# The residual of layer 1, turned in squares of 32 by VectorE at the end of layer 0, stored by token and loaded in rows

## The chip, the cores and the metric

The kernel runs on one core of one Trainium2 chip. The metric is the time of one execution on the device, in microseconds, as the median of several runs. Times that have a place in the program come from one profiled execution, and count from that execution's first instruction.

## The reference: two layers of a hybrid decoder trunk

1024 tokens with 1024 features pass through two layers. Layer 0 mixes the tokens by gated linear attention, layer 1 by a sparse attention in which an indexer picks 256 keys for each query. After each mixer the residual is added, normed, and given a gated term of its own:

```python
ALPHA = (2 * DEPTH) ** 0.25
...
for i in range(DEPTH):
    kind = i % N_MIXERS
    ...
    if kind == 0:
        y = gla_mixer(...)
    elif kind == 1:
        y = dsa_mixer(...)
    x = layer_norm(ALPHA * x + y, ln_g[i], ln_b[i])
    x = x + (p[i] @ ple_w[i]) * jax.nn.sigmoid(x @ ple_gate_w[i])
```

The change concerns the `x` that layer 0 leaves on this last line, and the term `ALPHA * x` of the line above it in layer 1. Both `dsa_mixer`'s output and the residual go into one sum per token, and `layer_norm` divides that sum by its own deviation, with a small constant under the root.

## The kernel before

**Tiling.** The tokens are worked on in two halves of 512 (`NH`, `HT`). The program is: layer 0 for the first half, layer 0 for the second, layer 1 for the first half, layer 1 for the second. An activation in "feature-major" form is eight tiles (`NK`) of 128 features x 512 tokens; these feed TensorE as operands. A matmul in near-f32 precision takes each operand as a high and a low part, which `split` makes: ScalarE copies a tile into the rounded type (the high part, L418), and VectorE subtracts that copy from the source (the low part, L410). A tile of `XT`, `x` in the profile's names, is such a pair. The sums that layer norm works on are "by token" instead: `y` is one tile of 128 tokens x 4 groups of tokens x 1024 features, so that a token's features lie in one partition. Going from the one form to the other needs a transposition.

**Layer 0's tail.** `tail` runs per half. It norms `y`, turns it back to feature-major tiles (`xpose`, TensorE, then L883 or L885), and then goes through eight gate blocks `b`, each 24 matmuls of 128x512 (`fm_block`). Behind a block, ScalarE applies the sigmoid, VectorE multiplies and adds (`gated`, L906 to L907), and `final` takes the finished feature-major tile `t` of layer 0's output. `final` (L1316) stores it into the DRAM tile `x2s` and splits it into the pair `X` that layer 1's first blocks read.

**Layer 1's residual.** Layer 1 runs in 16 slots per half, one for each head `h`, with matmul blocks of projections between the attention's own steps. In the slots 0 to 3 `residual` (L1442) loads two feature-major tiles back from `x2s` into `xst` tiles (256 KB each), lets TensorE transpose each in four 128x128 pieces into one PSUM bank (L1453, L62 in the profile), and lets ScalarE copy the bank into `y`, times `ALPHA` (L1454). After a slot's pair `st["y"]` counts up, and `dsa_out`, which adds the mixer's output into `y`, starts only when it has reached `NK` = 8. `norm_steps` then takes `y` with the constant `EPS`.

**What sets the order.** There is no scheduler: each engine runs its instructions in the order in which the Python program emits them. An object `fl` (`Flow`) keeps a modelled time `fl.now`, which every emitted matmul advances. Small steps are put on a heap with a due time (`fl.at`, `after`, and `chain`, a list of steps with the delay before the next), and are emitted between matmul blocks once their time has come. Two calls force what is on the heap out early: `fl.need(...)` emits steps until a condition holds, `fl.drain()` until the heap is empty. `fl.drain()` stands at the end of the second half's layer 0 (L1369); at the end of the first half there is none, and layer 1's small projections of that half (`small_head`) follow at once.

**What goes through SP.** All DMAs are issued by SyncE (SP) in program order. Of those that the prediction speaks of: `Weights` streams the weights' parts in (`whi` and `wlo` from `whs` and `wls`, L174); `split_ahead` (L213) prepares split weights in the background of layer 0, by a load of a raw piece `pst` (L223), ScalarE's copy `phi`, a store to `whs` (L235), VectorE's subtraction and a store to `wls` (L239), each store waiting for its engine; `small_head` loads the two rotary tables (L966 and L967, from `rope_s`; called `v` in the first half and `ix` in the second, by the tile that they take); L1644 loads the first half's keys `kI` in the second half.

**The rotary chain.** `small_head` projects the indexer's key and four blocks of its queries. `rope` turns each with the tables: two products and a shuffle on VectorE (L953 to L955), an addition (L958), then the split. Blocks of TensorE that use the results come some 40 us later.

Of the kernel before, what the change touches and what calls it, by code (L numbers as in the profile page):

```python
# [10 lines left out]
F32 = mybir.dt.float32  # L11
# [9 lines left out]
D = 1024  # L21
L = 1024
NH = 2
HT = 512
# [23 lines left out]
class Flow:  # L48
# [23 lines left out]
    def chain(self, *steps):  # L72

        (_, first), rest = steps[0], steps[1:]
        first()
        if rest:
            self.after(rest[0][0], lambda: self.chain((0, rest[0][1]), *rest[1:]))
# [200 lines left out]
def trunk_kernel(ctx, tc, x_tok, x_T, p_T, pos, freq, g_q, g_k, g_v, g_z, g_a, g_a2, g_ba, g_gn, g_o,  # L278
# [118 lines left out]

    x2s = dp.tile([NK, 128, L], F32, name="x2s")
    rope_s = dp.tile([4, 128, L], F32, name="rope_s")
    kv_s = dp.tile([6, 128, HT], F32, name="kv_s")  # L400
    sc_s = dp.tile([3, 128, L], F32, name="sc_s")

# [606 lines left out]
    def small_kv(half, X, f32t, alloc, tmp, spsum, kh, kl, vh, vl, res):  # L1009
        hs = slice(half * HT, half * HT + HT)  # L1010
        ch, sh = alloc(F32), alloc(F32)
        nc.sync.dma_start(ch[0:32], rope_s[0, 0:32, hs])
        nc.sync.dma_start(sh[0:32], rope_s[1, 0:32, hs])
        kf, vf = f32t(), f32t()

        def ev_k(ps):
            def done():
                res["k"] = True
            act.activation(kf, ps, AF.Copy)
            rope(kf[0:32], ch[0:32], sh[0:32], swap_h, tmp, lambda: split(kh, kl, kf, done))  # L1020

        yield from fm_block(("dk",), X, ev_k)

        def ev_v(ps):
            def turn():
                pt = spsum()
                for t in range(4):
                    fl.transpose(pt[:, t * 128:t * 128 + 128], vf[:, t * 128:t * 128 + 128], ident)

                def done():  # L1030
                    res["v"] = True
                split(vh, vl, pt, done)
            chain((0, lambda: act.activation(vf, ps, AF.Copy, scale=0.5)), (1.2, turn))

        yield from fm_block(("dv",), X, ev_v)

# [193 lines left out]
    for half in range(NH):  # L1230
# [82 lines left out]

        X = XT()

        def final(b, t, X=X, hs=hs):  # L1316
            nc.sync.dma_start(x2s[b, :, hs], t)
            X.put(b, t)
        turned = cycle((("U", 2), ("o", 1), ("U", 2), ("oT", 1), ("tr", 1)))

        def tps():
# [117 lines left out]
                X.put(*got)  # L1439
            yield  # L1440

    def residual(st, y, half, ks, start, end):  # L1442

        tiles = {}

        def load(k):
            tiles[k] = xp.tile([128, HT], F32, tag="xst", name="xst", bufs=2)
            nc.sync.dma_start(tiles[k], x2s[k, :, half * HT:(half + 1) * HT])

        def by_token(k):  # L1450
            ps = pbank()
            for t in range(4):
                fl.transpose(ps[:, t * 128:t * 128 + 128], tiles[k][:, t * 128:t * 128 + 128], ident)  # L1453
            act.activation(y[:, :, k * 128:k * 128 + 128], ps.rearrange("p (t c) -> p t c", c=128), AF.Copy,  # L1454
                           scale=ALPHA)
            st["y"] = k + 1

        for i, k in enumerate(ks):
            fl.at(start + 0.6 * i, lambda k=k: load(k))
            fl.at(end - 3.6 + 1.6 * i, lambda k=k: by_token(k))  # L1460

    def attend(st, h, half, ap, sq):

# [152 lines left out]
                                     [store(i) for i in range(nb)], [load(i) for i in range(nb)], [inverse, to_all])]  # L1616

    def dsa_out(st, js, ch, y, norm=None, ahead=1):
        fl.need(lambda: st.get("y") == NK)
        parts = [W.take(("do", j, ch)) for j in js]  # L1620

        def U(t, b):
# [78 lines left out]
    for half in range(NH):  # L1701
# [11 lines left out]
        for h, units in enumerate(plan, -1):  # L1713
# [36 lines left out]
            if h == 0:  # L1750
                y = xp.tile([128, 4, D], F32, tag="y", name="y")
            if 0 <= h < 4:
                residual(st, y, half, (2 * h, 2 * h + 1), start + 1.3, start + dur)
            fl.run(*(unit(u) for u in units))
        norm, y_done = norm_steps(y, l1, EPS, (0, 1))
        if half == 0:
            X = XT()
            feed_by(feed_x2(X, 1), fl.now + 21.0, 2.3)
# [80 lines left out]
```

## Time and profile before

| | before |
|---|---|
| time, median of 3 runs (lowest, highest) | 1962.26 us (1962.2, 1963.73) |
| the profiled execution, from its first to its last instruction | 1962.1 us |
| mean granted TensorE clock in it | 0.999 |
| HBM read, written | 331.18 MB, 131.99 MB |

The line of engines in the page (shown in the prediction) gives the busy time of each, with its share of the span. The page also cuts the span into 40 slices of 49 us; in each row a digit is the busy share in tenths, and the last two rows are the share of time in which the 16 DMA engines were busy and the rate at which they moved bytes:

```profile
PE   9999999999999999999999999999999999999999
DVE  5776676687778887877858987768797987777873
ACT  5664646446465646464545676766443553434432
DMA  4566565668757656656676588877866998888874
GB/s 153 185 184 212 190 215 181 215 183 263 249 186 236 210 194 195 211 180 209 209 260 250 181 309 289 275 264 267 317 216 234 362 317 295 297 302 276 291 272 145
```

Layer 0 ends for the first half at about 495 us (slice 11) and for the second at about 1025 us (slice 21); the residual's transposes in layer 1 lie between 1127 and 1593 us. TensorE is busy in every slice. In a row of a timeline, the columns are the start, the busy time, the engine, the line of the kernel, the operation, what it wrote and read, the tiles' shapes, and in brackets how long the engine had been idle before, and what ended that.

### The profile page before, as it was taken

How to read it: one execution, taken by the hardware profiler on the slowest of the kernel's cores; microseconds unless marked ns; L12 is line 12 of the kernel's file. 1: busy time of each engine (PE TensorE's matmuls, PEld its weight loads, DVE VectorE, ACT ScalarE, POOL GpSimd, SP SyncE). 2: the span in 40 equal slices, each digit the busy share in tenths (PEclk: the TensorE clock that was granted, in tenths of full speed). 3: DMA queues.
4: the chain of work that ended last, by engine and by line, in shares of the span. 5: the costliest groups of instructions: out<-in, count | busy, mean ns of one | idle time of the engine just before them, and what ended most of it. 6: DMA issues, size and time to landing. Idle time of an engine off the chain costs nothing.

```text
span 1962.1 us, 26826 instructions
## 1 busy us (share of the span) xinstructions
PE 1948.5 (99%) x9060; PEld 1614.2 (82%) x9060; DVE 1490.0 (76%) x3039; ACT 1021.7 (52%) x1928; POOL 53.6 (3%) x115
## 2 busy tenths in 40 slices
PE   9999999999999999999999999999999999999999
PEld 7888888888888888888888888888878888888877
DVE  5776676687778887877858987768797987777873
ACT  5664646446465646464545676766443553434432
POOL 0000000010000000000100000000000000000000
PEclk9999999999999999999999999999999999999999
DMA  4566565668757656656676588877866998888874
GB/s 153 185 184 212 190 215 181 215 183 263 249 186 236 210 194 195 211 180 209 209 260 250 181 309 289 275 264 267 317 216 234 362 317 295 297 302 276 291 272 145
DMA packets 174218, 464.96 MB, mean 237 GB/s; under 512 B 20096, under 2 KB 21120, under 8 KB 167936
## 3 DMA queue, kind: packets, MB, share of 16 engines
q1 hardware_dynamic: 174080, 463.25, 70.6%
q8 instruction: 71, 1.16, 0.2%
q14 instruction: 67, 0.55, 0.1%
HBM read 331.18 MB, written 131.99 MB: 236 GB/s over the span
## 4 chain that ended last, share of the span: by engine, by line
PE 93%; DVE 3%; ACT 2%; issue 1%; DMA 0%; SPq 0%; DVEq 0%; ACTq 0%
PE pb L58 70%; PE o L58 8%; PE U L58 6%; PE S L58 6%; PE oT L62 1%; PE tr L58 1%; DVE bn L828 0%; DVE y L786 0%; PE S L62 0%; ACT x L885 0%; DMA y<-in_x_T 0%; PE pb L62 0%; DVE sc L1067 0%; PE tr L62 0%; PE xt L62 0%
## 5 line engine op out<-in xcount | busy, mean ns | idle before, releaser
L58 PE MATMUL pb<-x,whi 128*128 128x512 f32 x2272 | 707.2, 392 | 0.0
L58 PEld LDWEIGHTS pb<-x,whi 128*128 128x128 f32 x2272 | 417.1, 188 | 79.5 <-DVE x L410 0.4
L58 PE MATMUL pb<-x,wlo 128*128 128x512 f32 x1136 | 443.1, 390 | 0.0
L58 PE MATMUL pb<-whi,u 128*128 128x512 f32 x1024 | 342.3, 394 | 0.1
L58 PEld LDWEIGHTS pb<-x,wlo 128*128 128x128 f32 x1136 | 213.3, 188 | 46.2 <-DVE wlo L191 0.4
L58 PEld LDWEIGHTS pb<-whi,u 128*128 128x128 f32 x1024 | 192.4, 188 | 40.8 <-ACT u L418 0.5
L58 PE MATMUL pb<-wlo,u 128*128 128x512 f32 x512 | 200.5, 392 | 0.0
L191 DVE TENSOR_TENSOR wlo<-wst,whi 128x512 fp32r<-128x512 f32 x232 | 154.5, 686 | 44.2 <-ACT whi L189 43.8
L189 ACT ACTIVATE whi<-wst 128x512 fp32r<-128x512 f32 x232 | 136.5, 622 | 81.7 <-DMA wst<-in_g_k 28.4
L1506 ACT ACTIVATE sq<-P,mx 128x128 f32<-128x128 f32 (+7 forms) x128 | 99.0, 774 | 89.3 <-DVE mx L1499 54.1
L1552 ACT ACTIVATE ph<-PT 128x512 fp32r<-128x512 f32 (+1 forms) x160 | 93.9, 601 | 63.5 <-PE o L58 44.6
L58 PE MATMUL S<-kT,q 128*128 128x512 f32 (+2 forms) x576 | 121.8, 343 | 0.0
L1550 DVE TENSOR_TENSOR PT<-PT,ph 128x512 fp32r<-128x512 f32 (+1 forms) x160 | 102.3, 649 | 17.7 <-ACT ph L1552 17.2
L58 PEld LDWEIGHTS S<-kT,q 128*128 128x128 f32 x576 | 100.5, 188 | 17.8 <-DVE mx L1499 0.7
L58 PEld LDWEIGHTS pb<-wlo,u 128*128 128x128 f32 x512 | 96.3, 188 | 18.8 <-DMA wlo<-wls 0.3
L1133 ACT ACTIVATE tk<-sc,tki 128x768 f16<-128x768 f32 (+2 forms) x90 | 92.8, 1031 | 22.9 <-DVE tki L1142 19.1
L58 PE MATMUL o<-ph,vT 128*128 128x512 f32 (+2 forms) x384 | 103.2, 353 | 0.2 <-ACT ph L1552 0.2
L1512 DVE STREAM_TRANSPOSE sq<-sq 128x128 f32<-128x128 f32 (+7 forms) x128 | 97.9, 769 | 4.0 <-ACT sq L1506 3.7
L731 ACT ACTIVATE junk<-o 128x512 bf16<-128x512 f32 x32 | 19.1, 597 | 152.1 <-DVE ot L729 141.0
L237 DVE TENSOR_TENSOR pst<-pst,phi 128x512 fp32r<-128x512 f32 x130 | 89.3, 687 | 5.4 <-ACT phi L233 5.0
L58 PE MATMUL pb<-whi,x 128*128 128x512 f32 x256 | 86.2, 395 | 0.4 <-DVE x L410 0.4
L58 PE MATMUL U<-whi,x 128*128 128x512 f32 x256 | 84.9, 391 | 0.0
(318 smaller groups left out, 3362.0 us busy)
## 6 DMA issues: line engine op xcount, KB each, us to landing
whi<-whs SPq DMA_DIRECT2D x128, 512.0 KB
wlo<-wls SPq DMA_DIRECT2D x128, 512.0 KB
sqd<-sq SPq DMA_DIRECT2D x192, 256.0 KB
PT<-sqd SPq DMA_DIRECT2D x48, 1024.0 KB
whs<-phi SPq DMA_DIRECT2D x130, 256.0 KB
wls<-pst SPq DMA_DIRECT2D x130, 256.0 KB
wst<-in_g_z SPq DMA_DIRECT2D x32, 512.0 KB
wst<-in_g_o SPq DMA_DIRECT2D x32, 512.0 KB
```

What stands on the lines that cost most here:

```text
L58: self.pe.matmul(out, lhsT, rhs, start=start, stop=stop)
L62: self.pe.transpose(out, in_, ident)
L189: self.nc.scalar.activation(hi[:, c], st[:, c], AF.Copy, scale=1.0 if gain is None else gain)
L191: self.nc.vector.tensor_sub(lo[:, c], st[:, c], hi[:, c].bitcast(F32))
L237: self.nc.vector.tensor_sub(st, st.bitcast(F32), hi.bitcast(F32))
L731: act.activation(junk, ps, AF.Square, accum_out=u["ss"][:, c:c + 1])
L1133: act.activation(junk()[:, :n], scs[j], AF.Sign, bias=cand[:, j:j + 1].bitcast(F32), accum_out=cnt[:, j:j + 1])
L1506: act.activation(to, rows, AF.Exp, scale=-1.0, bias=mx, accum_out=sm[:, t:t + 1])
L1512: dve.transpose(x, x)
L1550: dve.tensor_sub(lo, lo.bitcast(F32), hi.bitcast(F32))
L1552: chain((0, lambda: act.activation(hi, lo.bitcast(F32), AF.Copy)), (0.8, second))
```

## The change

In layer 0's tail, `final` now has a step more per tile. VectorE transposes the finished tile in squares of 32x32 into a tile `sq` (named `ah` in the profile, four buffers), and four DMAs store it to a new DRAM tile `yr_s`, by token. Squares alone do not transpose a tile: the rest is in the addresses of the stores, each of which takes 32 partitions (the tokens of one place in a square) with 16 pieces of 32 floats, and writes each piece into the row of its token. A store thus moves 64 KB in 512 pieces of 128 bytes. The turn has a due time 1.8 us of modelled time after `final`, the stores 2.2 us after the turn; both halves together have 16 turns and 64 such stores. The `x2s` store stays.

In layer 1, `residual` is now one load of 512 KB per slot 0 to 3, which brings 128 tokens' rows of 1024 features straight into `y`. The `xst` tiles, the 16 groups of four transposes and the 16 evictions are gone. `y` now holds `x` and not `ALPHA` times `x`; to make up for it, the values `V` are scaled by `0.5 / ALPHA` instead of 0.5, and the norm's constant is `EPS / ALPHA ** 2`. `dsa_out` starts when four loads are emitted.

```diff
--- before.py
+++ after.py
@@ -397,6 +397,7 @@
 
     x2s = dp.tile([NK, 128, L], F32, name="x2s")
     rope_s = dp.tile([4, 128, L], F32, name="rope_s")
+    yr_s = dp.tile([NH, 4, 4, 32, D], F32, name="yr_s")
     kv_s = dp.tile([6, 128, HT], F32, name="kv_s")
     sc_s = dp.tile([3, 128, L], F32, name="sc_s")
 
@@ -1030,7 +1031,7 @@
                 def done():
                     res["v"] = True
                 split(vh, vl, pt, done)
-            chain((0, lambda: act.activation(vf, ps, AF.Copy, scale=0.5)), (1.2, turn))
+            chain((0, lambda: act.activation(vf, ps, AF.Copy, scale=0.5 / ALPHA)), (1.2, turn))
 
         yield from fm_block(("dv",), X, ev_v)
 
@@ -1313,9 +1314,17 @@
 
         X = XT()
 
-        def final(b, t, X=X, hs=hs):
+        def final(b, t, X=X, hs=hs, half=half):
             nc.sync.dma_start(x2s[b, :, hs], t)
             X.put(b, t)
+            sq = t2k("ah", F32, 4)
+
+            def out():
+                for a in range(4):
+                    c = b * 128 + 32 * a
+                    nc.sync.dma_start(yr_s[half, :, :, :, c:c + 32].rearrange("t g c i -> c (t g) i"),
+                                      sq[32 * a:32 * a + 32].rearrange("p (n i) -> p n i", i=32))
+            chain((0, lambda: None), (1.8, lambda: dve.transpose(sq, t)), (2.2, out))
         turned = cycle((("U", 2), ("o", 1), ("U", 2), ("oT", 1), ("tr", 1)))
 
         def tps():
@@ -1439,25 +1448,12 @@
                 X.put(*got)
             yield
 
-    def residual(st, y, half, ks, start, end):
-
-        tiles = {}
-
-        def load(k):
-            tiles[k] = xp.tile([128, HT], F32, tag="xst", name="xst", bufs=2)
-            nc.sync.dma_start(tiles[k], x2s[k, :, half * HT:(half + 1) * HT])
-
-        def by_token(k):
-            ps = pbank()
-            for t in range(4):
-                fl.transpose(ps[:, t * 128:t * 128 + 128], tiles[k][:, t * 128:t * 128 + 128], ident)
-            act.activation(y[:, :, k * 128:k * 128 + 128], ps.rearrange("p (t c) -> p t c", c=128), AF.Copy,
-                           scale=ALPHA)
-            st["y"] = k + 1
-
-        for i, k in enumerate(ks):
-            fl.at(start + 0.6 * i, lambda k=k: load(k))
-            fl.at(end - 3.6 + 1.6 * i, lambda k=k: by_token(k))
+    def residual(st, y, half, t, start):
+
+        def load():
+            nc.sync.dma_start(y[:, t], yr_s[half, t].rearrange("g c d -> (g c) d"))
+            st["y"] = t + 1
+        fl.at(start, load)
 
     def attend(st, h, half, ap, sq):
 
@@ -1616,7 +1612,7 @@
                                      [store(i) for i in range(nb)], [load(i) for i in range(nb)], [inverse, to_all])]
 
     def dsa_out(st, js, ch, y, norm=None, ahead=1):
-        fl.need(lambda: st.get("y") == NK)
+        fl.need(lambda: st.get("y") == 4)
         parts = [W.take(("do", j, ch)) for j in js]
 
         def U(t, b):
@@ -1750,9 +1746,9 @@
             if h == 0:
                 y = xp.tile([128, 4, D], F32, tag="y", name="y")
             if 0 <= h < 4:
-                residual(st, y, half, (2 * h, 2 * h + 1), start + 1.3, start + dur)
+                residual(st, y, half, h, start + 1.3)
             fl.run(*(unit(u) for u in units))
-        norm, y_done = norm_steps(y, l1, EPS, (0, 1))
+        norm, y_done = norm_steps(y, l1, EPS / ALPHA ** 2, (0, 1))
         if half == 0:
             X = XT()
             feed_by(feed_x2(X, 1), fl.now + 21.0, 2.3)
```

**TensorE, slot 0 of layer 1 in the first half.** The rows are matmuls: `pb<-x,whi` and `pb<-x,wlo` are projections (PSUM bank from tile and weight), `pb<-ident,xst` the residual's transposes, `o<-...` the attention's output. Before:

```order
L58 MATMUL pb<-x,whi 128x512 x2
L58 MATMUL pb<-x,wlo 128x512
L62 MATMUL pb<-ident,xst 128x128 x4
L58 MATMUL o<-ph,vT_9810 128x512
L58 MATMUL o<-ph,vT_9811 128x512
L58 MATMUL o<-PT,vT_9810 128x512
L58 MATMUL pb<-x,whi 128x512 x2
L58 MATMUL pb<-x,wlo 128x512
L62 MATMUL pb<-ident,xst 128x128 x4
L58 MATMUL o<-ph,vT_9810 128x4x96
```

With the change:

```order
L58 MATMUL pb<-x,whi 128x512 x2
L58 MATMUL pb<-x,wlo 128x512
L58 MATMUL o<-ph,vT_9907 128x512
L58 MATMUL o<-ph,vT_9908 128x512
L58 MATMUL o<-PT,vT_9907 128x512
L58 MATMUL pb<-x,whi 128x512 x2
L58 MATMUL pb<-x,wlo 128x512
L58 MATMUL o<-ph,vT_9907 128x4x96
```

The two groups of transposes are gone, and the matmuls around them follow each other in the same order.

**SP, the end of the second half's layer 0.** The rows are DMAs in the order of issue: the weights of the last gate blocks, the stores of layer 0's last output tiles, then layer 1's first loads. Before:

```order
L174 DMA whi<-whs 128x1024
L174 DMA wlo<-wls 128x1024
L1317 DMA x2s<-x_9413 128x512
L1317 DMA x2s<-x_9423 128x512
L1644 DMA kI<-kv_s 128x512 x2
L966 DMA ix<-rope_s 128x512
L967 DMA ix<-rope_s 128x512
```

With the change:

```order
L174 DMA whi<-whs 128x1024
L174 DMA wlo<-wls 128x1024
L1325 DMA yr_s<-ah 32x16x32 x4
L1318 DMA x2s<-x_9462 128x512
L1318 DMA x2s<-x_9472 128x512
L1325 DMA yr_s<-ah 32x16x32 x8
L1640 DMA kI<-kv_s 128x512 x2
L967 DMA ix<-rope_s 128x512
```

The drain at L1369 brings out the stores of the last two tiles, eight in a row, between the last `x2s` store and the loads of `kI` and `ix`; the four of the tile before them stand ahead of the last two `x2s` stores.

**SP, the end of the first half's layer 0.** Here background stores and loads of `split_ahead` lie between the rest, and `v<-rope_s` is the rotary load. Before:

```order
L1317 DMA x2s<-x_4193 128x512
L235 DMA whs<-phi 128x512
L223 DMA pst<-in_d_z 128x512
L239 DMA wls<-pst 128x512
L174 DMA whi<-whs 128x1024
L174 DMA wlo<-wls 128x1024
L1317 DMA x2s<-x_4214 128x512
L235 DMA whs<-phi 128x512
L223 DMA pst<-in_d_z 128x512
L966 DMA v<-rope_s 128x512
```

With the change:

```order
L1325 DMA yr_s<-ah 32x16x32 x4
L1318 DMA x2s<-x_4194 128x512
L235 DMA whs<-phi 128x512
L223 DMA pst<-in_d_z 128x512
L239 DMA wls<-pst 128x512
L174 DMA whi<-whs 128x1024
L174 DMA wlo<-wls 128x1024
L1325 DMA yr_s<-ah 32x16x32 x4
L1318 DMA x2s<-x_4215 128x512
L235 DMA whs<-phi 128x512
L223 DMA pst<-in_d_z 128x512
L967 DMA v<-rope_s 128x512
```

A group of four turned stores now stands ahead of each `x2s` store from the second tile's on; six groups, 24 stores, come ahead of `v<-rope_s`, and the last two behind it.

## The prediction

> **What bounds the kernel now.** I read the page first, then the rows of the two edited places: TensorE's transposes in the first four slots of layer 1, and the end of layer 0 in each half with what follows it.
>
> ```profile
> span 1962.1 us, 26826 instructions
> PE 1948.5 (99%) x9060; PEld 1614.2 (82%) x9060; DVE 1490.0 (76%) x3039; ACT 1021.7 (52%) x1928; POOL 53.6 (3%) x115
> PE 93%; DVE 3%; ACT 2%; issue 1%; DMA 0%; SPq 0%; DVEq 0%; ACTq 0%
> ```
>
> TensorE is busy for 1948.5 of 1962.1 us and makes up 93% of the chain that ended last. So work taken from TensorE's stream comes off the time in full, and a delay elsewhere costs only what reaches TensorE. The sum is made against this execution's span of 1962.1 us; the median of the runs, 1962.26, lies 0.16 above it.
>
> **What is removed.** The first row counts the transposes of all residual tiles (minimum, median and largest duration in ns). The five after it are TensorE's timeline at the first and at the third residual group.
>
> ```profile
> L62 PE MATMUL pb<-ident,xst x64: 270/272/276, 1126.9 to 1593.3; 128*128 128x128 f32 x64
> ...
> 1126.68 0.39 PE L58 MATMUL pb<-x,wlo 128*128 128x512 f32 x1
> 1126.91 0.60 PE L62 MATMUL pb<-ident,xst 128*128 128x128 f32 x4
> 1127.26 0.72 PE L58 MATMUL o<-ph,vT 128*128 128x512 f32 x2
> ...
> 1143.00 0.60 PE L62 MATMUL pb<-ident,xst 128*128 128x128 f32 x4
> 1143.80 0.73 PE L58 MATMUL o<-ph,vT 128*128 128x512 f32 x2 [0.19 <-ACT ph L1552]
> ```
>
> The 272 ns of one transpose overlap with the next. What a group of four costs is the distance between the starts around it: 1127.26 - 1126.91 = 0.35 us. There are 64 / 4 = 16 groups, so TensorE's stream gets 16 x 0.35 = **5.6 us** shorter. At 1143.80 TensorE also sat idle for 0.19 us because ScalarE was late with `ph`; ScalarE's evictions of the residual, which go too, stand in front of it:
>
> ```profile
> L1454 ACT ACTIVATE y<-pb x16: 577/598/601, 1127.5 to 1593.6; 128x512 f32<-128x512 f32 x16
> L1512 DVE STREAM_TRANSPOSE sq<-sq 128x512 f32<-128x512 f32 x16 | 11.3, 707 | 3.6 <-ACT sq L1506 3.6
> ```
>
> I count 0.2 us for that. The rest of ScalarE's 16 x 0.598 = 9.6 us gives nothing, since ScalarE is busy for 52% of the span and TensorE does not wait for it there. Taken away in all: **5.8 us**.
>
> **What is added to VectorE.** 16 turns of 128x512. The second row has VectorE turning squares of that size in 707 ns, so 16 x 0.707 = 11.3 us. They fall into the last matmul blocks of layer 0:
>
> ```profile
> 455.00:460.00 5.00, 5.00 (x24) 4.14 (x23) 4.35 (x8) 3.67 (x6) 0.00 (x0) 1.00 0.71 247
> ...
> 493.00:498.00 5.00, 5.00 (x24) 4.14 (x23) 2.08 (x3) 0.97 (x2) 0.00 (x0) 1.00 1.02 356
> 500.00:510.00 10.00, 10.00 (x45) 8.26 (x44) 7.03 (x13) 3.58 (x6) 0.00 (x0) 1.00 1.03 404
> ```
>
> The third busy figure is VectorE's: 4.35 of 5 us at the start of the gate blocks, 2.08 at their end. One turn in each block of about 5.4 us fits into the idle rest, and each stands behind the low part that TensorE needs. VectorE's own time costs nothing. If it were full there, a turn would cost up to 0.7 us a block.
>
> **What is added to SP's queue, second half.** In the code each tile's four stores come late in the next block. At the end of the second half's layer 0 the program is drained: the turned stores of the last two tiles, eight in a row, come ahead of layer 1's first loads (the order's rows under the change). Before, SP and then VectorE and TensorE had there:
>
> ```profile
> 1017.54 5.76 SPq L1317 DMA_DIRECT2D x2s<-x  x2
> 1023.39 0.89 SPq L1644 DMA_DIRECT2D kI<-kv_s  x2
> 1024.33 0.42 SPq L966 DMA_DIRECT2D ix<-rope_s  x1
> ...
> 1023.65 0.69 DVE L410 TENSOR_TENSOR x<-x,x 128x512 fp32r<-128x512 f32 x1 [0.70 <-ACT x L418]
> 1029.41 0.68 DVE L953 TENSOR_TENSOR rt<-z,ix 64x512 f32<-64x512 f32 x1 [5.07 <-DMA ix<-rope_s]
> ...
> 1049.29 0.69 DVE L953 TENSOR_TENSOR rt<-z,ix 128x512 f32<-128x512 f32 x1 [0.19 <-ACT z L997]
> ...
> 1054.73 0.68 DVE L953 TENSOR_TENSOR rt<-z,qf 32x512 f32<-32x512 f32 x1 [0.55 <-ACT z L1019]
> ...
> 1070.49 0.69 DVE L410 TENSOR_TENSOR x<-y,x 128x512 fp32r<-128x512 f32 x1
> ...
> 1071.23 0.19 PEld L58 LDWEIGHTS pb<-x,whi 128*128 128x128 f32 x1 [0.36 <-DVE x L410]
> ...
> L1525 SPq DMA_DIRECT2D sqd<-sq x192: 303/601/1854, 1092.7 to 1869.3; - x192
> ```
>
> VectorE already waits 5.07 us for the rotary tables `ix`, whose load SP issues at 1024.33. With two `kI` issues in 0.89 us, one issue takes 0.45 us. The last tile's low part ends at 1023.65 + 0.69 = 1024.34 and its turn at 1025.05. The first four stores go from 1023.4 to 1025.2, the other four to 1027.0, so `kI` and then `ix` are issued 3.6 us later, and VectorE's wait ends 3.6 us later. What can take that up? Between 1029.41 and 1071 VectorE's only waits that are not part of the rotary chain itself are the 0.19 and the 0.55 us on ScalarE's evictions; of the 29 rows between 1054.73 and the low part at 1070.49 none has a wait. TensorE already waits 0.36 us for that low part. So 3.6 - 0.74 = **2.9 us** reach TensorE. From both sides: 0 if some of VectorE's queue can be caught up after all (the lag then ends in its idle time), and 4.1 with the 0.60 us median of the four-part stores `sqd<-sq` (8 x 0.6 = 4.8, less 0.74). I take 2.9 because the issue rows of that very place carry it.
>
> **Added to the DMA engines, first half.** Each store moves 64 KB as 32 x 16 pieces of 128 bytes, 32 pieces for each of 16 engines. No row shows a store in such pieces; the nearest is the small-piece loads at the kernel's start, in the stretch from 12.0 to 13.3 us:
>
> ```profile
> DMA packets 302, 0.10 MB, mean 77 GB/s; under 512 B 213, under 2 KB 280, under 8 KB 302
> ...
> q1 hardware_dynamic: 302, 0.10, 30.5%
> ...
> q1 hardware_dynamic: 174080, 463.25, 70.6%
> ...
> DMA packets 5290, 12.38 MB, mean 310 GB/s; under 512 B 590, under 2 KB 590, under 8 KB 5287
> ...
> SPq L223 <- DMA wls<-pst: 11.7, 6, 2.9
> ```
>
> 30.5% of 16 x 1.3 us over 302 packets is 21 ns each, with some 2-KB and larger ones in the mean: at most 32 x 0.021 = 0.67 us a store if a small store is like a small load. By bytes alone, at the 404 GB/s of the row of 500 to 510, it is 0.16 us. By the mean packet of the whole run (70.6% of 16 x 1962.1 us over 174080 = 127 ns) it is 4.1 us. I take **0.4 us**, the middle of the two nearest.
>
> The Trainium skill ("DMA: Bandwidth & Descriptors", "Specifications") says that transfers below 512 bytes miss the line rate because they are read, modified and written. If that doubled the 0.67 us, an estimate by this page, a store would take 1.3 us; no row of this trace shows a small store.
>
> 24 such stores stand ahead of the first half's rotary load (SP, 493 us): 24 x 0.4 = 9.6 us. The last but one row is the stretch from 460 to 500: 310 GB/s of the 404 seen, so 23% of the 33 us before 493, 7.7 us, are free, but SP spends 11.7 us of the same stretch (last row) waiting for a store of `wls` to land before it issues more, and a longer queue lengthens each of those waits. I count half of the free time and get a lag of 9.6 - 3.9, about 5.7 us at the worst and 1.9 at the best; I take 4.
>
> ```profile
> 498.81 0.68 DVE L953 TENSOR_TENSOR rt<-zz,v 64x512 f32<-64x512 f32 x1 [2.63 <-ACT zz L981]
> ...
> 504.74 0.69 DVE L953 TENSOR_TENSOR rt<-zz,v 128x512 f32<-128x512 f32 x1 [1.02 <-ACT zz L997]
> ...
> 510.18 0.69 DVE L953 TENSOR_TENSOR rt<-zz,v 128x512 f32<-128x512 f32 x1 [0.53 <-ACT zz L997]
> ...
> 515.62 0.69 DVE L953 TENSOR_TENSOR rt<-zz,v 128x512 f32<-128x512 f32 x1 [0.53 <-ACT zz L997]
> ...
> 521.06 0.69 DVE L953 TENSOR_TENSOR rt<-zz,v 128x512 f32<-128x512 f32 x1 [0.54 <-ACT zz L997]
> ...
> 541.24 0.73 PE L58 MATMUL ix<-v,u 128*128 128x512 f32 x2 [1.09 <-DVE v L410]
> ```
>
> Here the rotary chain waits for ScalarE, not for the tables, and the four waits from 504.74 on (1.02 + 0.53 + 0.53 + 0.54 = 2.6 us) take up lag. The remaining 1.4 us arrive at 541.24, where TensorE already waits 1.09 us for VectorE: **+1.4 us**, from 0 (0.16 us a store) to about 6 (0.67 us: 16.1 - 7.7 - 2.6).
>
> **The rest.** Eight loads of 512 KB take the place of sixteen of 256 KB: the same bytes. The factors 1/ALPHA cost nothing.
>
> **Sum.** 1962.1 - 5.6 - 0.2 + 2.9 + 1.4 = 1960.6 us, with the 0.16 a median of **1960.8**. The bounds of the two additions (0 to 4.1, 0 to 6) give 1956.5 to 1966.5 as this forecast's own range.
>
> **Rivals.** *A: both additions are covered.* For it: TensorE waits for almost nothing now, and the store pieces may be as cheap as bytes. Against it: the rows of 1029 to 1071 have no room. It gives 1962.26 - 5.8 = 1956.5.
>
> *B: slower, through the 128-byte pieces.* Everything SP loads goes through the same 16 engines behind these stores, weights too. At 0.67 us a store, the first half loses 6 us as above; in the second, 32 x 0.67 = 21.4 us meet a stretch that moves about 275 GB/s of 404 for 38 us (32% free, 12 us), so `ix` lands 9.4 + 2.9 = 12 us late. That is -5.8 + 6 + 12 = +12, **1974 us**. At 1.3 us a store both halves lose 20 to 30 us, and it is 2007. It decides from about 0.45 us a store, where the losses equal 5.8. For it: the 93% DMA share of 460 to 500 (row below); against it: the 21 ns are a ceiling for loads. The skill's rule on 512 bytes, above, is the page that speaks for this rival.
>
> *C: the row loads collide.* In the second half's first slots of layer 1 the DMA engines are full, and a 512-KB load now stands ahead of `PT`, where 256 KB stood:
>
> ```profile
> q1 hardware_dynamic: 5287, 12.35, 93.0%
> ...
> 1540.00:1560.00 20.00, 20.00 (x101) 16.79 (x100) 17.25 (x36) 11.45 (x23) 0.00 (x0) 1.00 0.99 333
> ```
>
> 256 KB at 404 GB/s are 0.65 us in each of four slots: 2.6 us, hence 1963.4. TensorE is busy for all 20 us there, so `PT` has some slack, which speaks against it.
>
> **How the numbers follow.** Forecast 0.40, A 0.24, B 0.31, C 0.05. This kernel's measurement can tell about 0.2%, 3.9 us, from no change. A is faster by more; the forecast and C lie within; B is slower; a little of the forecast falls outside on either side: faster 0.26, same 0.42, slower 0.32. The range from 1956.0 to 1976.0 leaves out the dearer half of B and a trace below A, about 0.18.
>
> **What would show it.** Right: no `pb<-ident,xst`; a wait of about 8.7 us of VectorE for `ix` near 1033; TensorE waiting some 3 us for an `x` tile near 1074; a packet row with 32768 more under 512 bytes and their time near 12 ns each. Wrong: `ix` no later (A), or waits of TensorE for `whi` and `wlo` from DMA in the first half near 490 to 515 (B). The four stores' issue time on SP is the number I trust least after the piece's own.

## The result, and the profile after

| | before | with the change |
|---|---|---|
| median of 4 runs each | 1962.23 us | 1982.88 us (1982.18 to 1984.92) |
| ratio, 95% interval | | 1.0104 [1.0092, 1.0116] |
| span of the profiled execution | 1962.1 us | 1980.7 us |

The change costs 20.6 us. The page of the changed kernel, with the lines that answer to those of before:

```profile
span 1980.7 us, 26783 instructions
PE 1951.0 (98%) x8996; PEld 1608.9 (81%) x8996; DVE 1500.2 (76%) x3055; ACT 1012.3 (51%) x1912; POOL 53.6 (3%) x115
...
DMA packets 206858, 469.16 MB, mean 237 GB/s; under 512 B 53760, under 2 KB 54784, under 8 KB 200576
...
PE 80%; DVE 9%; ACT 4%; DMA 4%; issue 2%; SPq 1%; ACTq 0%; DVEq 0%
```

TensorE has its 64 matmuls fewer, VectorE its 16 instructions more, and the packets under 512 bytes grew by 33,664 (20,096 before), of which the stores' pieces are 64 x 512 = 32,768; the rest are packets of 4 bytes, 16 for each of the 56 DMAs more. The chain that ended last, 93% TensorE before, is now 80%: VectorE, ScalarE and the DMA engines have taken most of the difference over.

**Where the time went.** But for the residual's transposes both kernels run the same 8996 matmuls in the same order. So the start of the k-th in one trace can be set against the k-th in the other; the difference is called the lag here, and what it grows by in a stretch is what that stretch lost. (Every place is given by before's time.) All traces but two start with a lag of about -2 us, since TensorE ran at half clock for a moment in before's own start-up (the profile's windows; the third figure from the end is the granted clock):

```profile
16.00:18.00 2.00, 2.00 (x7) 1.51 (x6) 1.75 (x4) 1.15 (x2) 0.00 (x0) 0.52 0.79 258
18.00:20.00 2.00, 2.00 (x7) 1.62 (x6) 0.81 (x2) 0.27 (x1) 0.00 (x0) 0.63 0.24 61
```

That is 2 x 0.48 + 2 x 0.37 = 1.7 us, and no part of the change. The growth of the lag, for the changed kernel and the experiments told below, each from one traced execution:

| kernel | end of layer 0, first half (455 to 600) | end of layer 0, second half (1020 to 1110) | layer 1 (1110 to 1955) |
|---|---|---|---|
| the change | +12.3 | +8.9 | -0.5 |
| no_stores | 0.0 | 0.0 | +1.3 |
| one_plain | 0.0 | +1.4 | +0.8 |
| four_plain | +2.0 | +3.3 | +0.1 |
| two_and_half_plain | +7.3 | +4.2 | 0.0 |
| one_in_pieces | +13.0 | +8.2 | -0.2 |
| act_queue | +13.5 | +9.1 | -1.0 |
| pool_queue | +25.2 | +33.4 | +0.2 |
| plain_then_gather | +0.5 | +1.1 | +20.4 |
| gather_clock | 0.0 | +2.4 | +25.5 |
| late_scatter | 0.0 | +1.1 | +1.1 |
| no_stores_clock | 0.0 | 0.0 | -1.3 |
| before_no_clock | 0.0 | 0.0 | +3.2 |
| no_stores_no_loads | 0.0 | 0.0 | -3.1 |
| after_clock | +10.7 | +9.3 | -1.9 |

The change loses 21.2 us at the two ends of layer 0, and layer 1, where 5.6 us of transposes are gone, gives back 0.5.

**How the end of the first half goes now.** The DMA queue in the stretch from 460 to 500 us (packets, MB, share of the 16 engines):

```profile
q1 hardware_dynamic: 15942, 11.11, 99.6%
```

SP's timeline there (start, time, what it issued; rows left out are marked):

```profile
485.69 3.69 SPq L1325 DMA_DIRECT2D yr_s<-ah  x4
489.47 2.52 SPq L1318 DMA_DIRECT2D x2s<-x  x1
...
502.45 0.45 SPq L967 DMA_DIRECT2D v<-rope_s  x1
```

The engines went from 93.0% to 99.6%. SP needs 3.69 + 2.52 = 6.2 us for four turned stores and the one store behind them, in a block of 5.4 us (6.7 for the group at 494.59, but 2.6 for the one at 480.24), and issues the rotary load at 502.45, 9.2 us later than before. What that does on VectorE, in its timeline, one row for each half:

```profile
506.42 0.68 DVE L954 TENSOR_TENSOR rt<-zz,v 64x512 f32<-64x512 f32 x1 [12.00 <-DMA v<-rope_s]
...
1049.14 0.68 DVE L954 TENSOR_TENSOR rt<-z,ix 64x512 f32<-64x512 f32 x1 [13.98 <-DMA ix<-rope_s]
```

And TensorE's timeline in the first half:

```profile
509.05 0.73 PE L58 MATMUL pb<-x,whi 128*128 128x512 f32 x2 [1.91 <-DMA whi<-whs]
510.28 0.50 PE L58 MATMUL pb<-x,wlo 128*128 128x512 f32 x1 [0.49 <-DMA wlo<-wls]
510.61 0.63 PE L58 MATMUL pb<-x,whi 128*128 128x512 f32 x2
511.08 0.47 PE L58 MATMUL pb<-x,wlo 128*128 128x512 f32 x1
511.35 1.05 PE L58 MATMUL pb<-x,whi 128*128 128x512 f32 x2
```

VectorE waits 12.0 and 14.0 us for the rotary tables (0 and 5.1 before), and TensorE waits for weights, which it did not before. TensorE's waits by releaser in the changed kernel (total, times, longest) show that VectorE's wait is not the main way to it:

```profile
PE pb L58 <- DMA whi<-whs: 2.8, 2, 1.9
PE ix L58 <- ACT rl L1072: 2.7, 1, 2.7
PE S L62 <- ACT z L982: 2.4, 1, 2.4
PE S L58 <- ACT rt L1072: 1.9, 2, 1.6
PE ix L58 <- DVE v L411: 1.5, 1, 1.5
PE pb L58 <- DMA wlo<-wls: 1.4, 3, 0.5
```

The rows of `whi`, `wlo`, `rl` and `v` lie in the first half, those of `z` and `rt` in the second. Before, there were 1.1 us for `v`, 0.3 for `rt` and nothing for the other four. So the rotary chain's own row in the first half, `v`, grew by 0.4 us. The 2.7 us for `rl` come from another late load: ScalarE, ahead of `rl` in its order, stood 7.00 us until 532.92 for a piece of raw weights (`wst`), which SP issued at 524.1 in place of 511.9.

In the rows of 509 to 512, two matmuls behind a wait of 1.91 us take 1.05 us in place of 0.63. The windows show why:

```profile
510.00:512.00 2.00, 1.72 (x6) 1.42 (x7) 1.97 (x5) 1.15 (x2) 0.00 (x0) 0.81 1.32 179
512.00:514.00 2.00, 2.00 (x6) 1.51 (x6) 1.93 (x4) 0.00 (x0) 0.00 (x0) 0.50 0.77 155
514.00:516.00 2.00, 2.00 (x9) 1.63 (x8) 1.27 (x3) 1.80 (x3) 0.00 (x0) 0.84 1.06 422
```

The granted clock falls to 0.50 and comes back: (0.19 + 0.50 + 0.16) x 2 = 1.7 us. The changed kernel has two such falls at the first half's end and one at the second's, 5.1 us of the 21.2.

### The profile page after: what moved, and what is told of

Same layout as the page of the kernel before. It is cut to its first block, busy times and chain, and to the rows that moved or that the text cites. A ratio compares the mean times of both kernels' runs of the same rounds, so it can differ in the third digit from the quotient of the medians.

```text
span 1980.7 us, 26783 instructions
## 1 busy us (share of the span) xinstructions
PE 1951.0 (98%) x8996; PEld 1608.9 (81%) x8996; DVE 1500.2 (76%) x3055; ACT 1012.3 (51%) x1912; POOL 53.6 (3%) x115
## 4 chain that ended last, share of the span: by engine, by line
PE 80%; DVE 9%; ACT 4%; DMA 4%; issue 2%; SPq 1%; ACTq 0%; DVEq 0%
PE pb L58 60%; PE o L58 7%; PE U L58 6%; PE S L58 5%; DMA PT<-sqd 1%; PE oT L62 1%; PE tr L58 1%; DVE sc L1068 1%; DVE sq L1508 1%; DVE rt L955 1%; DVE y L787 1%; DVE PT L1546 1%; DVE bn L829 0%; DVE rt L956 0%; PE S L62 0%
```

## The experiments

In the runs that leave the turned stores out or put other stores in their place (`no_stores`, `no_stores_clock`, `four_plain`, `one_in_pieces`, `one_plain`, `two_and_half_plain`), `y` reads rows of the kernel's input, so that nothing depends on what is stored. `act_queue` and `pool_queue` change only which engine issues.

### Which property of the stores costs: four runs

`no_stores` (the load is the same in the next three):

```diff
-                for a in range(4):
-                    ...dma_start(yr_s[half, :, :, :, c:c + 32]..., sq[32 * a:32 * a + 32]...)
+                pass
...
-            nc.sync.dma_start(y[:, t], yr_s[half, t].rearrange("g c d -> (g c) d"))
+            nc.sync.dma_start(y[:, t], x_tok[half * HT + t * 128:half * HT + t * 128 + 128, :])
```

> The changed kernel without its 64 turned stores; the turns on VectorE stay, and the eight row loads of y read rows of the kernel's input x_tok instead (same bytes, same pieces), so the residual's values are other ones. In the changed kernel's trace TensorE lies 12 us further behind at the end of the first half's layer 0 and 9 us at the end of the second's than before, and layer 1, where 5.6 us of transposes are gone, gains only 0.4. Both theories of the stores (their number in SP's queue, or their 128-byte pieces) expect the two lags to be gone, within 1 us. The two theories of layer 1 differ. If the gain of layer 1 is given back because the attention's own chain (stores of sq, load of PT, parts) ends last there, whatever layer 0 did, it stays at 0 to 1.5 us and the span is 1961 to 1963. If it was lost only since layer 0's delay had shifted the work, layer 1 now gains 5 to 6 us, and the span is 1955.5 to 1957.5.

Measured: 1961.79 us, ratio 0.9993 [0.9981, 1.0004]. Both lags are gone, so the stores make all of them, and VectorE's 16 turns nothing. In the trace layer 1 even loses 1.3 us, though its transposes are gone and nothing delayed it; but the traced execution was the slowest of eight, 1.5 us above their median, so the loss is not typical. What stands is that the gain is not shifted away by layer 0: something in layer 1 eats it.

`four_plain`, `one_in_pieces` and `one_plain`:

```diff
+                for a in range(4):
+                    nc.sync.dma_start(yr_s[half, b, 32 * a:32 * a + 32], sq[32 * a:32 * a + 32])
...
+                nc.sync.dma_start(yr_s[half, b, :, :, 0:32], sq.rearrange("p (n i) -> p n i", i=32))
...
+                nc.sync.dma_start(yr_s[half, b], sq)
```

> As the run without stores, but with four stores of 64 KB per tile to a scratch tile, each of 32 partitions with one piece of 2 KB: as many stores as in the changed kernel and as many bytes, but 32 pieces for 512. If the number of issues in SP's queue is the cause (eight DMAs in flight, 4 to 6 us from issue to landing, four more of them in each block of 5.4 us), the lags stay near 12 and 9 us, and the span is 16 to 22 us above the run without stores. If the 128-byte pieces are the cause, the lags are 0 to 4 us in each half, and the span is 0 to 6 us above it.

> As the run without stores, but with one store of 256 KB per tile to a scratch tile, of 128 partitions with 16 pieces of 128 bytes each that don't touch: the pieces and bytes of the changed kernel's four stores in one issue. If the pieces are the cause, the lags stay near 12 and 9 us, and the span is 16 to 22 us above the run without stores. If the number of issues is the cause, the lags are 0 to 4 us in each half.

> As the run without stores, but with one store of 256 KB per tile to a scratch tile, in 128 pieces of 2 KB. Both theories expect little: 0 to 3 us above the run without stores. If it is the bytes alone that cost (4.2 MB, 0.65 us per tile at 404 GB/s), it lies as far above as the two other runs.

Measured: 1969.70 us, 1.0033 [1.0022, 1.0044]; 1982.27 us, 1.0096 [1.0066, 1.0125]; 1964.81 us, 1.0008 [0.9997, 1.0019]. At layer 0's ends the same bytes cost 1.4 us in one plain store, 5.3 in four, and 21.2 in one store of 128-byte pieces, as much as the changed kernel's four (the two runs of `one_in_pieces` lie 4.6 us apart). So it is the pieces; the number of issues adds a few us, the bytes little.

### Do pieces cost by the engines' time, or by holding up SP's queue?

`act_queue` and `pool_queue` let another engine issue the stores:

```diff
-                    nc.sync.dma_start(yr_s[...
+                    nc.scalar.dma_start(yr_s[...      # act_queue; nc.gpsimd in pool_queue
```

> The changed kernel with the 64 turned stores issued by ScalarE instead of SP; the pieces, the bytes and the addresses are the same. Theory E (the DMA engines are the limit: 24 stores of 0.42 us in a stretch where they are 93% busy): SP's loads are issued sooner but land later behind the same pieces, the lags at the ends of layer 0 stay at 8 us or more in each half, and the span is 1975 to 1985. Theory Q (SP's queue is the limit: what stands behind a store with 512 pieces is issued up to 3 us late, while the engines could have taken it): the lags fall to 0 to 3 us in each half, and the span is 1960 to 1967.

Measured: 1983.66 us, 1.0107 [1.0087, 1.0127]. The lags stay, but for another reason: TensorE now waits for ScalarE, which stands behind its own stores. The waits by releaser (total, times, longest):

```profile
PE pb L58 <- ACT x L419: 13.3, 4, 6.6
```

ScalarE's own timeline has one group of four stores in front of such a copy (4.25 us of issuing):

```profile
501.46 4.25 ACTq L1325 DMA_DIRECT2D yr_s<-ah  x4
505.76 0.63 ACT L419 ACTIVATE x<-x 128x512 fp32r<-128x512 f32 x1 [7.46 <-issue]
```

Behind these waits the granted clock stood at 0.50 for 20.5 us, against 10.2 in the changed kernel. So the run does not tell the theories apart. But it shows the stores on a queue of their own, from 460 to 500 us:

```profile
q1 hardware_dynamic: 4390, 10.36, 72.8%
q10 hardware_dynamic: 12657, 1.57, 25.0%
```

25.0% of 16 x 40 us over 12,657 packets is 12.6 ns a piece, 32 x 12.6 = 0.40 us a store on 16 engines. In the changed kernel's own trace, on SP's queue, the packets of 128 bytes took 12.8 ns.

> The changed kernel with the 64 turned stores issued by GpSimd, which is 3% busy, instead of SP; pieces, bytes and addresses are the same. The run with ScalarE as issuer did not tell its two theories apart, since ScalarE itself stood up to 7.5 us behind its stores, and TensorE waited for ScalarE. Theory E (the DMA engines are the limit): SP's issues are no longer late, but its loads land later; TensorE waits for weights and for the rotary chain, the lags at the ends of layer 0 are 6 us or more in each half, and the span is 1973 to 1985. Theory Q (what stands behind a store in SP's queue is the limit): the lags are 0 to 3 us in each half, and the span is 1960 to 1967.

Measured: 2022.34 us, 1.0301 [1.0257, 1.0345]. Undecided again. GpSimd's stores go one at a time, so the four `sq` tiles come free late, and VectorE stands still for them (groups of VectorE by shape, 455 to 530 us; the last figure is its idle time before them):

```profile
L1327 DVE STREAM_TRANSPOSE ah<-x 128x512 f32<-128x512 f32 x8 | 5.6, 706 | 31.5 <-DMA yr_s<-ah 31.5
```

`two_and_half_plain` puts the same time on the engines without the pieces:

```diff
+                nc.sync.dma_start(yr_s[half, b, 0], sq)
+                nc.sync.dma_start(yr_s[half, b, 1], sq)
+                nc.sync.dma_start(yr_s[half, b, 2, 0:64], sq[0:64])
```

> As the run with one plain store per tile (y reads rows of x_tok, so the residual's values are other ones), but with three stores per tile to a scratch tile, of 256, 256 and 128 KB in pieces of 2 KB. At 404 GB/s they take 640 KB / 404 = 1.6 us of the DMA engines, as the changed kernel's four stores do (4 x 0.42 = 1.7 us), in 320 pieces for 2048 and in three issues for four. Theory E (the engines' time is the limit): the lags at the ends of layer 0 are as in the changed kernel, 7 to 13 us in each half, and the span is 1975 to 1985. Theory Q (the pieces hold up SP's queue): the lags lie between those of one plain store and of four (0 to 2 and 1 to 3.5 us), and the span is 1962 to 1968.

The engine time did come out alike: between 460 and 500 us a packet of 2 KB took 89 ns in the mean, so the 320 of a tile take 1.8 us of 16 engines, and the four stores of pieces 4 x 0.40 = 1.6.

Measured: 1973.19 us, 1.0055 [1.0032, 1.0078], between the two theories. The lags are 7.3 and 4.2 us; one fall of the clock, in the first half, is 1.7 of them. Without such falls it stands so:

| | the change | the same engine time, plain |
|---|---|---|
| first half | 12.3 - 3.4 = 8.9 | 7.3 - 1.7 = 5.6 |
| second half | 8.9 - 1.7 = 7.2 | 4.2 |

So the engines' time alone makes about 60% of the waiting (`after_clock` below, with the same stores as the change, waited 2.3 us longer, which makes it a little over half), and the rest goes with the pieces. A mechanism for that rest shows in SP's rows: a group of four turned stores and the `x2s` store behind it took 6.2 us of SP at 485.69 in the changed kernel, and this is what the run has there:

```profile
485.07 0.68 SPq L1323 DMA_DIRECT2D yr_s<-ah  x1
485.81 0.70 SPq L1324 DMA_DIRECT2D yr_s<-ah  x1
486.56 0.71 SPq L1325 DMA_DIRECT2D yr_s<-ah  x1
487.74 0.33 SPq L1318 DMA_DIRECT2D x2s<-x  x1
```

2.4 us. That issuing itself is held up by pieces is measured; that this alone is the rest is inferred.

### Is it the place?

`plain_then_gather` moves the pieces to the loads, `late_scatter` to copies from DRAM to DRAM, spread over the second half's layer 0 and layer 1's first half:

```diff
+                nc.sync.dma_start(yr_s[half, b], sq)                       # plain_then_gather
...
+            for g in range(4):
+                n = (4 * t + g) * 32
+                nc.sync.dma_start(y[32 * g:32 * g + 32, t]..., yr_s[half, :, :, n:n + 32]...)
...
+                nc.sync.dma_start(yr_p[half, b], sq)                       # late_scatter
...
+            nc.sync.dma_start(yr_s[half, :, :, :, c:c + 32]..., yr_p[half, b, 32 * a:32 * a + 32]...)
+        for i in range(32):
+            fl.at(start + gap * i, lambda i=i: one(i // 4, i % 4))
```

> The changed kernel with the 128-byte pieces moved from the stores to the loads: each turned tile is stored in one plain store of 256 KB with pieces of 2 KB, and each of the slots 0 to 3 of layer 1 gathers its rows in four loads of 128 KB with pieces of 128 bytes. If the loss of the changed kernel comes from the pieces at layer 0's end, where the DMA engines were 93% busy, the two lags there fall to 0 to 2 us. In layer 1 the pieces take 4 x 1024 x 13 ns / 16 = 3.3 us of the DMA engines per slot instead of some 1.2; if PT is late by that, up to 2 us per slot come back in the second half, where the engines are 99% busy. Span 1962 to 1970; 1980 if the place of the pieces does not matter.

Measured: 1984.85 us, 1.0117 [1.0088, 1.0147]. Layer 0's ends are clean, as expected; layer 1 loses 20.4 us, far more than the 8 allowed for. The granted clock stood at 0.50 for 10.2 us of it. TensorE waits there for ScalarE's copies of `PT`, which are loaded behind the gathers:

```profile
PE o L58 <- ACT ph L1548: 11.7, 5, 5.6
PE o L58 <- DVE PT L1546: 5.9, 7, 2.9
```

> The changed kernel with the modelled time kept as the transposes kept it, and with the 128-byte pieces moved to quieter stretches: each turned tile is stored plainly (256 KB, pieces of 2 KB), and 64 copies of 64 KB from DRAM to DRAM, one in each 7 to 10 us, put the pieces in rows, for the first half during the second half's layer 0, for the second half during layer 1's first half. The result is that of the reference. If the changed kernel's loss is one of the place (the 128-byte pieces on DMA engines that are 93% busy, ahead of loads that are waited for), the lags at layer 0's ends are those of the run with one plain store (0 to 1.5 us), the copies cost 0 to 3 us, and the span is 1959 to 1964. If the pieces cost wherever they are, it is 1972 to 1982.

Measured: 1963.65 us (10 runs), 1.0001 [0.9992, 1.0011]. The first half's copies cost nothing: the lag stands at -2.5 us at 600 and at 1020. The second half's cost 2.4 us in layer 1 (+1.1, against the -1.3 of `no_stores_clock` below), and the plain stores 1.1. By the medians, each against the runs of before beside it, the two together cost 1.9 us. So the same 32,768 pieces cost some 2 us where hardly anything waits behind them, and some 20 at layer 0's ends. The copies are also spread thinner, one in 7 to 9.5 us for four in 5.4, so the run does not tell place and density apart. This is the best form of the whole change that was run, and it is no faster than before.

### Why layer 1 does not get its 5.6 us

`no_stores_clock` keeps the modelled time, and `before_no_clock` takes it out of the kernel before:

```diff
+        def tick():
+            fl.now += 4 * 0.109
+        for i in range(2):
+            fl.at(end - 3.6 + 1.6 * i, tick)
...
+            fl.now -= 4 * 0.109        # before_no_clock: in by_token, behind the transposes
```

> The run without stores, plus one step in the place of each group of four transposes that only advances the modelled time fl.now by the same 4 x 0.109 us as the transposes did. With it every instruction on VectorE and ScalarE of layer 1 is emitted in the order of before again; without it the rotary steps and others come ahead of the low part that TensorE waits for. As there, y reads rows of x_tok, so the residual's values are other ones. Theory 1 (the 5.6 us were given back because removing the transposes also took them out of the modelled time, which reordered VectorE and ScalarE): layer 1 now gains 5 to 6 us, the span is 1955.5 to 1957.5, about 5 below the run without stores. Theory 2 (the attention's chain of stores, loads and parts ends last there whatever the order): no change against the run without stores, within 1 us.

> The kernel before, with the transposes and evictions of the residual, but with the modelled time set back by 4 x 0.109 us after each group of four, so that VectorE and ScalarE get the changed kernel's order in layer 1 and every engine still does the same work. Theory 1 (order): TensorE waits 4 to 6 us more in layer 1, the span is 1966 to 1968. Theory 2 (the attention's chain ends last once the transposes are gone): within 1 us of before, since nothing is gone.

Measured: 1961.18 us, 0.9996 [0.9985, 1.0007], and 1965.31 us, 1.0014 [1.0003, 1.0025]. In the kernel before, where no work is removed at all, the order costs 2.8 us by the medians and 3.2 in the trace. Without the stores the traces differ by 1.3 + 1.3 = 2.6 us, but the medians do not separate the two: each against the runs of before beside it, `no_stores` gains 1.2 us and `no_stores_clock` 1.3. In the kernel before that is about half of what theory 1 wanted: the order is one cause and not the whole.

The lags show where. At 15 of the 16 removed groups the changed kernel's lag falls at once, by some 0.36 us (0.80 at one), so the transposes were worth about what they were priced at. It rises by 1.2, 1.9 and 1.2 us at 1133, 1193 and 1363 us, in the changed kernel, in `no_stores` and in `before_no_clock` alike, and at none of the three in `no_stores_clock` and `after_clock`, where the time is kept. There TensorE loses 0.9, 1.1 and 1.0 us at 1130, 1407 and 1409 us instead. What the first of the three places looks like, in VectorE's timeline before:

```profile
1131.64 0.69 DVE L1607 TENSOR_TENSOR uf<-o,z 128x512 f32<-128x512 f32 x1 [1.28 <-PE o L58]
1132.25 0.68 DVE L410 TENSOR_TENSOR q<-qf,q 128x512 fp32r<-128x512 f32 x1
1132.85 0.67 DVE L953 TENSOR_TENSOR rt<-qf,tab 32x512 f32<-32x512 f32 x1
```

And in `no_stores`, in the timeline of all engines (the fifth row is the low part of `q`):

```profile
1128.38 0.67 DVE L953 TENSOR_TENSOR rt<-qf,tab 32x512 f32<-32x512 f32 x1
...
1129.00 0.72 DVE L954 STREAM_SHUFFLE rt<-qf 32x512 f32<-32x512 f32 x1
1129.75 0.68 DVE L955 TENSOR_TENSOR rt<-rt,tab 32x512 f32<-32x512 f32 x1
1130.36 0.67 DVE L1599 TENSOR_TENSOR uf<-o,z 128x512 f32<-128x512 f32 x1
1130.96 0.67 DVE L410 TENSOR_TENSOR q<-qf,q 128x512 fp32r<-128x512 f32 x1
...
1131.69 0.74 PE L58 MATMUL S<-kT,q 128*128 128x256 f32 x4 [1.06 <-DVE q L410]
```

The three rotary steps of the next tile now stand ahead of `uf` and of `q`'s low part, and TensorE waits 1.06 us for that part.

`no_stores_no_loads` drops the row loads too, with the time kept:

```diff
-            nc.sync.dma_start(y[:, t], x_tok[...])
+                pool.memset(y, 0.5)
```

> The run without stores and with the modelled time kept, and without the eight row loads of y too: GpSimd sets y to 0.5, so the residual is a constant. With the order kept, layer 1 gained 1.3 us of the 5.6 in the trace. Theory L (the row loads of 512 KB take up the rest, by delaying PT on full DMA engines): layer 1 now gains 4 to 6 us, the span is 1954.5 to 1957. Theory S (the attention's chain sets the pace in these slots whatever is loaded): layer 1 gains 1 to 2.5 us, the span is 1957.5 to 1959.5.

Measured: 1960.08 us, 0.9988 [0.9978, 0.9999]. Layer 1 gains 3.1 us, between the theories: the row loads cost 1.8, and of 5.6 us another 2.5 are eaten even so. Most of that goes at one place, at the end of layer 1's first half:

```profile
1404.71 0.69 DVE L1593 TENSOR_TENSOR z<-z,inv 128x512 f32<-128x512 f32 x1 [1.88 <-DMA inv<-row]
1405.32 0.68 DVE L1547 TENSOR_TENSOR PT<-PT,ph 128x512 fp32r<-128x512 f32 x1
1406.06 0.19 PEld L58 LDWEIGHTS o<-PT,vT 128*128 128x128 f32 x1 [1.81 <-DVE PT L1547]
```

TensorE comes earlier by what was saved, and waits 1.81 us for a low part that stands on VectorE behind a product that waits for a DMA.

`after_clock` is the changed kernel with the same `tick` steps.

> The changed kernel with the step that advances the modelled time as the transposes did; the result is that of the reference. If the changed order of VectorE and ScalarE costs 2.8 to 3.4 us there too, as in the traces without stores and of the kernel before, the lag grows by that much less from 1110 us on: the span is 1977 to 1978.5, against 1980.7 of the changed kernel. If layer 1's loads set the pace after the delay anyway, it is 1980 to 1981.

Measured: 1979.31 us, 1.0086 [1.0057, 1.0115], span 1978.1 us. Layer 1 gains 1.9 us in place of 0.5, so the order is worth 1.4 there, less than expected. The rest of the span's difference is at layer 0's ends, where nothing was edited: the clock fell once in place of three times (3.4 us less), and the waits were 2.3 us longer.

`gather_clock` is `plain_then_gather` with the same steps. It was expected to be 4 to 6 us faster than that run if the order costs (theory 1), and as fast if it does not (theory 2). Measured: 1988.18 us, 1.0134 [1.0105, 1.0164], 3.3 us slower by two runs each. In its trace the granted clock stood at 0.50 for 20.5 us of layer 1, twice as long as in the other's. It bears out neither theory, and what the order is worth can't be read from it.

## Why the prediction was wrong, point by point

**The price of a store was right**, in part by luck: 0.4 us was taken as the middle between 0.16 and 0.67, without a row of such a store, and 0.40 was measured. VectorE's turns took 702 to 706 ns, as taken, and none waited.

**The step that failed is how much of it the DMA engines could take up in the first half.** "310 GB/s of the 404 seen, so 23% of the 33 us before 493, 7.7 us, are free" counts bytes. The row that stood under rival C had the same stretch at 93.0% busy, which leaves 7% of 33 = 2.3 us: at 310 GB/s and 93.0% busy, full engines would have moved some 333 GB/s there, and not 404. With it, 24 x 0.4 - 2.3 = 7.3 us would have been the lag of the loads, and not 4. Measured were 9.2 us on SP's clock, 11.6 against TensorE, which was 2.4 us ahead of before by then. Behind it two terms were missing: SP's own issuing, held up to 6.7 us a block, and a path. The sum let the lag reach TensorE through the rotary chain alone, where it added 0.4 us; TensorE's waits for `whi` and `wlo` added 4.2, and the one for `rl` behind late raw weights 2.7. The term was +1.4 us; it measured 12.3, of which the falls of the clock are 3.4.

**In the second half only the last eight issues were counted.** SP issues `ix` at 1044.4 in place of 1024.3 (the issue's duration in ns, three times, then its start, twice):

```profile
L967 SPq DMA_DIRECT2D ix<-rope_s x1: 430/430/430, 1044.4 to 1044.4; - x1
```

Of the 20.0 us, 10.2 are TensorE's lag by then, so 9.8 are new, and 3.6 were forecast. The eight stores alone took 5.5 us of SP, 0.69 each for the 0.45 taken, and the groups before them delayed the queue too. VectorE's wait is 14.0 us, against the 8.7 named as a sign. The other sign, TensorE waiting some 3 us for an `x` tile near 1074, did not come: its waits for `x` tiles there add up to 0.3 us. Of the 8.9 us that the term of +2.9 measured, 2.6 were lost at 1040 in a way that the prediction does not have: ScalarE's copy `z`, which TensorE needs, had waited 5.82 us for an `x2s` store. The fall of the clock behind it is 1.7, and the other 4.6 came after 1057, mostly in waits for `rt` and `z`, which ScalarE makes between its steps of the rotary chain.

**"Work taken from TensorE's stream comes off the time in full"** failed too: -5.8 us forecast, -0.5 measured in layer 1. The prediction looked for moved instructions at layer 0 alone; each group of transposes also carried 0.44 us of modelled time, and their removal reordered VectorE and ScalarE in layer 1 (2.8 us by the medians in the kernel before, 1.4 in the changed kernel's traces). The row loads, rival C, cost 1.8 us (2.6 in its sum), and 2.5 us at most are lost to chains that were as late as TensorE. Even with neither stores nor loads the change was worth 3.1 us, not 5.8.

**Rival B was the case**, by its sign (waits of TensorE for `whi` and `wlo`, at 509 to 525) and, for the share that goes with the engines' time, by its mechanism. Its point, "about 0.45 us a store", was too high by the same error; it took place at 0.40. Its own time, 1974 us at the dearer 0.67 us a store, still fell 9 us short: SP's issuing and the falls of the clock are not in it. The 512-byte rule of the Trainium skill ("DMA: Bandwidth & Descriptors", "Specifications") agrees in direction: 64 KB in such pieces take 0.40 us of the engines, and 0.16 by the rate of 404 GB/s.

## What to carry to other kernels

Whether a queue has room is read from the busy share of its engines and from what the issuing queue waits for, not from bytes per second; small pieces fill engines at a low rate. Where a program's order comes from a modelled clock, removed work also removes its time from that clock: keep the time, compare the order on every engine, and only then credit the saving. Transfers in small pieces belong where nothing that is waited for stands behind them, even if that takes a further copy.

## What was not expected of the hardware

**A wait of TensorE costs more than itself.** Idle times of 1.9 to 3.2 us between TensorE's matmuls were followed by a stretch at a granted clock of 0.50 in 8 of the 9 cases of four traces (the change, `after_clock`, `one_in_pieces`, `two_and_half_plain`). Seven of these falls cost 1.7 us each, and the one in the second half of `one_in_pieces` lasted twice as long; an idle time of 2.65 us in `after_clock` had none, nor had one of 2.93 us in `plain_then_gather`.

So the length of the wait alone does not decide. Within a trace the changes of the granted clock lie on one grid with steps of 3.41 us: the changed kernel's falls begin at 511.24, 535.13 and 1040.31 us, 7 and 148 steps apart, and each lasts one step. In the step ahead of each of the 23 falls of all 16 traces, TensorE's matmuls were busy for 5 to 52% of the time (50, 21 and 29% for those three); in every other step at full clock, from 12 us on, for 50% or more (the ends of matmuls are modelled, so 2% of overlap say little). The 2.65 us lay across two steps that were 54 and 68% busy, the 2.93 us across two at 54%. By these traces a wait costs more than itself where it leaves TensorE idle for half of one step; that this is the rule is inferred.

The Trainium skill ("TensorE: Matmul & The Clock Gate", "The HAM clock gate (the "warmup" mystery)") has half rate until some 3.4 us of work, which agrees with 1.7 us lost; it asks for an idle window of about 3.4 us, and here a step that was half idle was enough, as the one with most of the wait of 1.91 us was.

**GpSimd's stores** of the same pieces came out as other packets. The queues of `pool_queue`, over the whole trace:

```profile
q1 hardware_dynamic: 172928, 463.25, 68.2%
q0 software_dynamic: 2048, 4.20, 0.8%
```

2,048 packets for 64 stores are 32 each; by the trace's sizes 16 of them hold 4 KB and 16 hold 4 bytes. They took 4.2 us of the engines a store, 0.26 on 16, against 0.40 from ScalarE's queue. Yet the stores went one at a time, 2.4 us or more from one issue to the next. Why was not tried.
